# A quarter of the block copies behind VectorE's 32 by 32 transposes moves to GpSimd, in a hybrid decoder block

## The chip, the core and the metric

The kernel runs on one core of a Trainium2 chip (trn2). The metric is the device time of one execution in microseconds (us); of the kernel before, three runs are known (2516.44, 2516.70 and 2517.51), and one execution was taken with a profile. A core has TensorE (PE in the rows, its weight loads PEld), VectorE (DVE), ScalarE (ACT), GpSimd (POOL) and SyncE (SP), each with a queue of its own that it works through in order. A queue waits for another by semaphores.

## The reference

One decoder layer over 512 positions of width 2048, in float32:

```python
h = rmsnorm(x, norm_mix_g)
qa, ka, va, qb, kb, vb, ga, gb = split(h @ w_in)
ya = sliding_window_attention(qa, ka, va, sinks) @ w_branch_a    # window 128, 16 heads over 4 groups
yb = stick_breaking_attention(qb, kb, vb) @ w_branch_b           # strictly causal, 16 heads
x = x + (sigmoid(ga) * ya + sigmoid(gb) * yb) @ w_out
x = x + swiglu(rmsnorm(x, norm_ffn_g))
out = rmsnorm(x, norm_final_g)
```

Both attentions work in 128 by 128 blocks: a block of weights (query by key) has to be turned (key by query) before TensorE can multiply it with the values. The turning is what the change touches.

## The kernel before, in words

Every float32 product is made of three fp32r products: both factors are split into a high part (ScalarE casts it) and a low part (VectorE subtracts). For the weights this is `Weights.parts`: L153 casts a loaded chunk `raw` to `whi` on ScalarE, L154 makes `wlo` on VectorE. Three buffers of each let the two engines run up to two chunks ahead of TensorE; the cast of a chunk waits until TensorE has released the buffer. TensorE's stream of large products (lines L343 to L345 in the first half) is the main work. After each piece of it, `gap()` takes a waiting closure from the list `pieces`, so that the attention's small steps are written between the large products; `pace` says how many per piece. The final order on each engine is set by a scheduler that runs when the program is built and works from its own cost estimates, so a changed engine for one instruction can move others.

The first attention (`unit_a`, the stretch from about 105 to 370 us) has 28 turns of four 128 by 128 blocks: two `nc.vector.transpose` (L650) write `z`, in which every 32 by 32 block is turned in itself but still stands at its old place. `unblock` (L588 to L597) then makes 16 copies of 32 partitions each, which put the blocks in their place in `turned`. `split_turned` casts `turned` to `ph` (ScalarE, L601) and subtracts to get `pl` (VectorE, L602), and TensorE multiplies them with the values (L661, L662). Behind the last of these units TensorE goes on with the second attention: this is the hand-over, near 350 us.

The second attention (`head_b`, about 360 to 840 us) has 16 heads. `scores` makes sigmoids on ScalarE, two masks on GpSimd (`strictly_before`, L713), a scan and a product on VectorE; `turn(j)` transposes 4, 3, 2 or 1 blocks (L756), calls `unblock` with n = 4 to 1, casts to `ath` or `corner` (L601) and subtracts (L602); `values` are the products at L770 to L774. For the last group `pace` is raised, so that the pieces are done when the gates are: the heads stand closer together from about 750 us on.

A third user, `turn_x1` (L874), turns twelve column blocks of the residual (four blocks each) while the next product of the output matrix runs, about 1080 to 1185 us.

Which engine makes a copy is decided in `unblock`: of 16 copies `share` go to ScalarE, the others to VectorE. `share` is 10 in `unit_a` and 8 elsewhere:

```python
copy = nc.scalar.copy if (i + 1) * share // 16 > i * share // 16 else nc.vector.tensor_copy
copy(t4[c * Q : (c + 1) * Q, :, r], z4[r * Q : (r + 1) * Q, :, c])
```

Of the kernel before, what the change touches and what calls it, by code (L numbers as in the profile page):

```python
# [45 lines left out]
def kernel(  # L46
# [15 lines left out]
    nc = tc.nc  # L62
# [21 lines left out]
    def slot(s, dt=F32, w=T):  # L84
        return tp.tile([P, w], dt, tag="t", name=uid(s))
# [502 lines left out]
    def unblock(z, n, share):  # L588

        t = slot("turned")  # L590
        z4 = z[:, : n * P].rearrange("p (n c q) -> p n c q", n=n, c=4)
        t4 = t[:, : n * P].rearrange("p (n r q) -> p n r q", n=n, r=4)
        for i in range(16):
            r, c = i // 4, i % 4
            copy = nc.scalar.copy if (i + 1) * share // 16 > i * share // 16 else nc.vector.tensor_copy
            copy(t4[c * Q : (c + 1) * Q, :, r], z4[r * Q : (r + 1) * Q, :, c])  # L596
        return t  # L597

    def split_turned(z, n, hi, lo, share):
        t = unblock(z, n, share)[:, : n * P]  # L600
        nc.scalar.copy(hi, t)  # L601
        nc.vector.tensor_tensor(out=lo, in0=t, in1=f(hi), op=ALU.subtract)  # L602
# [271 lines left out]
    def turn_x1(k, xr, tag):  # L874

        g = gcol[:, KD + k : KD + k + 1]
        if k < KD - 4:
            z = slot("z")
            for t in range(NT):
                nc.vector.transpose(z[:, t * P : (t + 1) * P], xr[t][:, (k % 4) * P : (k % 4 + 1) * P])  # L880
            v = unblock(z, NT, 8)
            nc.scalar.activation(out=v, in_=v, func=AF.Copy, scale=g)
        else:
            b = bank(tag)
            for t in range(NT):
                transpose(b[:, t * P : (t + 1) * P], xr[t][:, (k % 4) * P : (k % 4 + 1) * P])
            v = slot("turned")
            nc.scalar.activation(out=v, in_=b, func=AF.Copy, scale=g)
        xs2[k] = v
        if k % 2 and k < KD // 2 + 2:  # L890
            forms_of(k // 2)
# [249 lines left out]
```

## Time and profile before

| | |
|---|---|
| median of three runs | 2516.7 us |
| the profiled execution, its own time | 2515.71 us |
| its span, first to last instruction | 2513.6 us |
| TensorE busy | 2472.4 us, 98% of the span |
| VectorE busy | 1977.8 us, 79% |
| ScalarE busy | 1377.9 us, 55% |
| GpSimd busy | 256.4 us, 10% |
| mean granted TensorE clock | 0.994 |
| copies of L596 | 888 on ScalarE, 776 on VectorE |

A row of a group gives the line, engine, operation and tiles, the count, the busy time, the mean duration of one in ns, and the idle time of the engine just before, with what ended it. In a timeline row the bracket holds the idle time before it and its releaser. TensorE's share says how much of the span it had a product in flight; where it waited, and for whom, stands in the list of waits.

### The profile page before, as it was taken

What the parts mean: (1) busy time and instruction counts of PE and PEld (TensorE: products, weight loads), DVE (VectorE), ACT (ScalarE), POOL (GpSimd) and SP (SyncE); (2) the same over time, 40 slices, a digit from 0 to 9 for tenths busy, and PEclk for the clock granted to TensorE, in tenths of its full rate; (3) what the DMA queues carried; (4) which work ended last, traced back from release to release, by engine and by line L of the source; (5) the groups of instructions that cost most, each with busy time, mean ns of one, the idle gap of its engine ahead of it and who ended that gap; (6) DMA issues with size and microseconds to landing.
All of it is one profiled execution on the core that took longest, in us unless ns stands there. A gap on an engine that the chain in (4) does not pass through costs nothing.

```text
span 2513.6 us, 33228 instructions
## 1 busy us (share of the span) xinstructions
PE 2472.4 (98%) x11529; PEld 2063.3 (82%) x11529; DVE 1977.8 (79%) x3457; ACT 1377.9 (55%) x2627; POOL 256.4 (10%) x490
## 2 busy tenths in 40 slices
PE   9999999999999999999999999999999999999997
PEld 8888978888887788888788888888888877888886
DVE  5688888988769644376788888888888878888888
ACT  6567776766657533265554555545555444333345
POOL 0000001111101000000000011000110033302100
PEclk9999999999999999999999999999999999999999
DMA  5332333333323644454456656566565699958652
GB/s 177 93 101 91 101 101 103 104 98 103 108 88 104 202 149 144 133 161 134 150 165 193 197 170 184 169 193 190 176 184 168 191 334 322 315 161 277 190 186 85
DMA packets 255784, 408.00 MB, mean 162 GB/s; under 512 B 16480, under 2 KB 103552, under 8 KB 255616
## 3 DMA queue, kind: packets, MB, share of 16 engines
q1 hardware_dynamic: 200944, 302.03, 38.7%
q0 software_dynamic: 47552, 91.25, 11.6%
q10 hardware_dynamic: 7120, 12.61, 1.3%
q8 instruction: 90, 1.47, 0.2%
q14 instruction: 78, 0.64, 0.1%
HBM read 344.48 MB, written 61.34 MB: 161 GB/s over the span
## 4 chain that ended last, share of the span: by engine, by line
PE 50%; issue 12%; POOL 2%; DVE 2%; DMA 1%; ACT 0%; POOLq 0%; DVEq 0%
PE mm L261 7%; PE mm L260 7%; PE mm L259 6%; PE at L260 5%; PE at L261 5%; PE at L259 5%; PE mm L345 3%; PE mm L343 3%; PE mm L344 3%; POOL fx L1031 2%; PE at L860 1%; PE mm L861 1%; PE mm L860 1%; PE at L861 1%; PE at L859 1%
## 5 line engine op out<-in xcount | busy, mean ns | idle before, releaser
L153 ACT CAST whi<-wx 128x1024 fp32r<-128x1024 f32 x256 | 269.6, 1053 | 306.5 <-PE mm L261 132.0
L260 PE MATMUL mm<-wlo,fx 128*128 128x512 f32 x1056 | 413.7, 392 | 1.1 <-DVE wlo L154 1.1
L261 PE MATMUL mm<-whi,fx 128*128 128x512 f32 x1056 | 411.9, 390 | 0.0
L154 DVE TENSOR_TENSOR wlo<-raw,whi 128x1024 fp32r<-128x1024 f32 (+1 forms) x209 | 253.7, 1215 | 186.1 <-ACT whi L153 184.4
L154 DVE TENSOR_TENSOR wlo<-wx,whi 128x1024 fp32r<-128x1024 f32 x256 | 312.6, 1222 | 80.5 <-ACT whi L153 80.1
L259 PE MATMUL mm<-whi,fx 128*128 128x512 f32 x1056 | 369.4, 390 | 0.4 <-ACT whi L153 0.4
L153 ACT CAST whi<-wz 128x1024 fp32r<-128x1024 f32 x198 | 207.7, 1054 | 281.1 <-PE at L261 111.4
L345 PE MATMUL mm<-fh,wlo 128*128 128x512 f32 x896 | 351.3, 392 | 3.8 <-DVE wlo L154 3.7
L343 PE MATMUL mm<-fh,whi 128*128 128x512 f32 x896 | 351.3, 392 | 0.0
L344 PE MATMUL mm<-fl,whi 128*128 128x512 f32 x896 | 351.0, 392 | 0.0
L153 ACT CAST whi<-raw 128x1024 fp32r<-128x1024 f32 (+1 forms) x209 | 218.2, 1046 | 222.9 <-PE mm L344 126.8
L260 PE MATMUL at<-wlo,fx 128*128 128x512 f32 x792 | 311.7, 394 | 4.1 <-DVE wlo L154 4.1
L261 PE MATMUL at<-whi,fx 128*128 128x512 f32 x792 | 309.6, 391 | 0.0
L596 ACT COPY turned<-z 32x128 f32<-32x128 f32 (+3 forms) x888 | 242.4, 273 | 110.3 <-DVE z L756 60.7
L154 DVE TENSOR_TENSOR wlo<-wz,whi 128x1024 fp32r<-128x1024 f32 x198 | 240.1, 1222 | 60.1 <-ACT whi L153 60.1
L259 PE MATMUL at<-whi,fx 128*128 128x512 f32 x792 | 277.9, 391 | 2.6 <-ACT whi L153 2.6
L260 PEld LDWEIGHTS mm<-wlo,fx 128*128 128x128 f32 x1056 | 198.6, 188 | 43.1 <-DVE wlo L154 2.2
L259 PEld LDWEIGHTS mm<-whi,fx 128*128 128x128 f32 x1056 | 198.0, 188 | 42.5 <-ACT whi L153 1.3
L261 PEld LDWEIGHTS mm<-whi,fx 128*128 128x128 f32 x1056 | 198.6, 188 | 40.9
L345 PEld LDWEIGHTS mm<-fh,wlo 128*128 128x128 f32 x896 | 169.3, 189 | 41.0 <-DVE wlo L154 5.5
L344 PEld LDWEIGHTS mm<-fl,whi 128*128 128x128 f32 x896 | 169.5, 189 | 33.4
L343 PEld LDWEIGHTS mm<-fh,whi 128*128 128x128 f32 x896 | 169.4, 189 | 33.1
(261 smaller groups left out, 4184.6 us busy)
## 6 DMA issues: line engine op xcount, KB each, us to landing
raw<-in_w_in_dram SPq DMA_DIRECT2D x135, 512.0 KB, 3.6
wz<-in_w_ffn_in_dram SPq DMA_DIRECT2D x88, 512.0 KB, 4.4
raw<-in_w_ffn_in_dram SPq DMA_DIRECT2D x83, 512.0 KB, 3.7
wx<-in_w_ffn_in_dram SPq DMA_DIRECT2D x49, 512.0 KB, 4.2
raw<-in_w_ffn_down_dram SPq DMA_DIRECT2D x44, 512.0 KB, 4.2
wz<-in_w_ffn_down_dram SPq DMA_DIRECT2D x44, 512.0 KB, 5.7
raw<-in_w_out_dram SPq DMA_DIRECT2D x32, 512.0 KB, 3.7
wx<-in_w_ffn_down_dram SPq DMA_DIRECT2D x22, 512.0 KB, 7.1
```

Of the source, the lines that this page charges most:

```text
L153: self.cast = nc.scalar.copy(hi[:, :n], raw[:, :n])
L154: nc.vector.tensor_tensor(out=lo[:, :n], in0=raw[:, :n], in1=f(hi[:, :n]), op=ALU.subtract)
L259: mm(banks[t], lhsT=hi, rhs=wh[:, kk, :], start=one, stop=False, skip_group_check=True)
L260: mm(banks[t], lhsT=hi, rhs=wl[:, kk, :], start=False, stop=False, skip_group_check=True)
L261: mm(banks[t], lhsT=lo, rhs=wh[:, kk, :], start=False, stop=end, skip_group_check=True)
L343: mm(b, lhsT=wh[:, kk, c], rhs=hi[k], start=(k == 0), stop=False)
L344: mm(b, lhsT=wh[:, kk, c], rhs=lo[k], start=False, stop=False)
L345: mm(b, lhsT=wl[:, kk, c], rhs=hi[k], start=False, stop=(k == nk - 1))
L596: copy(t4[c * Q : (c + 1) * Q, :, r], z4[r * Q : (r + 1) * Q, :, c])
L860: mm(banks[t], lhsT=hi[k][:, c], rhs=wl[:, kk, :], start=False, stop=False)
L861: mm(banks[t], lhsT=lo[k][:, c], rhs=wh[:, kk, :], start=False, stop=(k == nk - 1))
L1031: nc.gpsimd.dma_start(out=res[i][name], in_=form_d[p0 + i][name])
```

## The change

Of the 16 copies of a turn, the four with `i % 4 == n % 4` go to GpSimd, where `n` is the number of 128 by 128 blocks. As `i % 4` is the column of 32 in which the block stands in `z`, these are the four copies of one column.

```diff
         for i in range(16):
             r, c = i // 4, i % 4
             copy = nc.scalar.copy if (i + 1) * share // 16 > i * share // 16 else nc.vector.tensor_copy
+            if i % 4 == n % 4:
+                copy = nc.gpsimd.tensor_copy
             copy(t4[c * Q : (c + 1) * Q, :, r], z4[r * Q : (r + 1) * Q, :, c])
```

With `share` 10 and n = 4 (`unit_a`) GpSimd takes two copies of ScalarE's ten and two of VectorE's six. With `share` 8 the even `i` are VectorE's: n = 4 and n = 2 take four of VectorE's eight, n = 3 and n = 1 four of ScalarE's eight.

ScalarE at the hand-over, behind the splitting of the last keys of the first group (`kh`): the copies and casts of the last three turns of the first attention. Before:

```order
L509 CAST kh_3697<-v_3689 64x512
L153 CAST whi_3850<-raw_3848 128x1024
L596 COPY turned_3722<-z_3717 32x4x32 x10
L601 CAST ph_3720<-turned_3722 128x512
L664 COPY tmp_3758<-at_3753 64x512
L153 CAST whi_3904<-raw_3902 128x1024
L596 COPY turned_3787<-z_3782 32x4x32 x10
L601 CAST ph_3785<-turned_3787 128x512
```

Now (the lines behind the change are two higher):

```order
L509 CAST kh_3697<-v_3689 64x512
L153 CAST whi_3850<-raw_3848 128x1024
L598 COPY turned_3722<-z_3717 32x4x32 x8
L603 CAST ph_3720<-turned_3722 128x512
L666 COPY tmp_3758<-at_3753 64x512
L153 CAST whi_3904<-raw_3902 128x1024
L598 COPY turned_3787<-z_3782 32x4x32 x8
L603 CAST ph_3785<-turned_3787 128x512
```

Nothing changes its place here; two copies of ten are gone from each turn.

VectorE near the end of the second attention, from the low part of one weight chunk (`wlo_8640`) on. Before:

```order
L154 TENSOR_TENSOR wlo_8640<-raw_8637,whi_8639 128x1024
L602 TENSOR_TENSOR corner_2785<-turned_8536,corner_2784 128x128
L749 TENSOR_TENSOR a_8595<-a_8595,fl_8596 128x511
L602 TENSOR_TENSOR atl_8617<-turned_8618,ath_8616 128x512
L756 STREAM_TRANSPOSE z_8674<-a_8458 128x128
L756 STREAM_TRANSPOSE z_8674<-a_8402 128x128
L756 STREAM_TRANSPOSE z_8674<-a_8337 128x128
L154 TENSOR_TENSOR wlo_8729<-raw_8726,whi_8728 128x1024
L596 COPY turned_8680<-z_8674 32x3x32 x3
L748 SCALAR_TENSOR_TENSOR fl_8659<-fl_8659 128x384
L596 COPY turned_8680<-z_8674 32x3x32 x5
```

Now:

```order
L154 TENSOR_TENSOR wlo_8640<-raw_8637,whi_8639 128x1024
L604 TENSOR_TENSOR atl_8617<-turned_8618,ath_8616 128x512
L758 STREAM_TRANSPOSE z_8674<-a_8458 128x128
L758 STREAM_TRANSPOSE z_8674<-a_8402 128x128
L758 STREAM_TRANSPOSE z_8674<-a_8337 128x128
L750 SCALAR_TENSOR_TENSOR fl_8659<-fl_8659 128x384
L598 COPY turned_8680<-z_8674 32x3x32 x7
L751 TENSOR_TENSOR a_8658<-a_8658,fl_8659 128x383
L598 COPY turned_8680<-z_8674 32x3x32
L154 TENSOR_TENSOR wlo_8729<-raw_8726,whi_8728 128x1024
```

The next low part, `wlo_8729`, went from the place ahead of the eight copies to the place behind them and behind a scan.

ScalarE at the last head of the second attention (the turn into `turned_9121` is its first, with four blocks). Before:

```order
L596 COPY turned_9064<-z_9062 32x32 x8
L776 COPY tmp_9098<-at_9089 64x512
L601 CAST corner_2784<-turned_9064 128x128
L153 CAST whi_9142<-raw_9140 128x1024
L596 COPY turned_9121<-z_9114 32x4x32 x8
L781 DMA y_526<-yb_8842 128x512
L601 CAST ath_9119<-turned_9121 128x512
```

Now:

```order
L598 COPY turned_9064<-z_9062 32x32 x4
L603 CAST corner_2784<-turned_9064 128x128
L778 COPY tmp_9098<-at_9089 64x512
L598 COPY turned_9121<-z_9114 32x4x32 x8
L783 DMA y_526<-yb_8842 128x512
L153 CAST whi_9142<-raw_9140 128x1024
L603 CAST ath_9119<-turned_9121 128x512
```

The cast of the weight chunk moved from ahead of the eight copies to the place between them and the cast `ath` that the turn ends in.

## Rows read from the trace of the kernel before

**Rows 1.** Busy time by stretch: the stretch (us from the span's start), its length, busy us (and instructions) of PE, PEld, DVE, ACT and POOL, then the granted TensorE clock, the DMA share and GB/s. The hand-over, the middle and the end of the second attention, and the stage behind it with `turn_x1`.
```profile
315.00:370.00 55.00, 48.87 (x205) 38.91 (x204) 44.61 (x109) 41.26 (x100) 0.00 (x0) 0.97 0.28 87
...
370.00:750.00 380.00, 380.00 (x2002) 329.04 (x2001) 315.83 (x808) 251.36 (x656) 55.52 (x104) 1.00 0.33 104
...
750.00:840.00 90.00, 84.07 (x362) 67.95 (x361) 80.90 (x246) 65.13 (x192) 11.73 (x24) 0.94 0.31 100
...
840.00:1200.00 360.00, 360.00 (x1590) 298.10 (x1589) 195.03 (x418) 164.19 (x298) 6.62 (x12) 1.00 0.48 155
```

**Rows 2.** The waits of TensorE over the whole span, those of the first 840 us: who waited for whom, us in total, times, the longest.
```profile
PE at L661 <- ACT ph L601: 4.2, 1, 4.2
...
PE mm L345 <- DVE wlo L154: 3.7, 3, 1.8
...
PE at L773 <- ACT corner L601: 1.9, 2, 1.5
...
PE at L773 <- DVE corner L602: 1.2, 1, 1.2
...
PE at L662 <- DVE pl L602: 0.8, 1, 0.8
```

**Rows 3.** Timeline of the hand-over (start, us, engine, line, operation, tiles, count), ACT, DVE and the one long wait of PE.
```profile
338.40 3.07 ACT L596 COPY turned<-z 32x128 f32<-32x128 f32 x10 [2.76 <-DVE z L650]
...
341.49 1.05 ACT L153 CAST whi<-raw 128x1024 fp32r<-128x1024 f32 x1
...
342.57 1.23 DVE L154 TENSOR_TENSOR wlo<-raw,whi 128x1024 fp32r<-128x1024 f32 x1 [2.80 <-ACT whi L153]
...
353.03 0.77 DVE L650 STREAM_TRANSPOSE z<-s 128x256 f32<-128x256 f32 x2
...
353.73 1.18 DVE L154 TENSOR_TENSOR wlo<-raw,whi 128x1024 fp32r<-128x1024 f32 x1
...
353.83 3.06 ACT L596 COPY turned<-z 32x128 f32<-32x128 f32 x10 [1.00 <-DVE z L650]
...
356.92 0.62 ACT L601 CAST ph<-turned 128x512 fp32r<-128x512 f32 x1
...
357.59 0.80 PE L661 MATMUL at<-ph,vv 128*128 128x512 f32 x1 [4.18 <-ACT ph L601]
```

**Rows 4.** Timeline of the end of the second attention: a stall of TensorE at a weight chunk, with POOL.
```profile
796.38 1.42 POOL L713 TENSOR_SCALAR_AFFINE_SELECT a<-a 128x128 f32<-128x128 f32 x1
...
796.53 1.18 DVE L748 TENSOR_TENSOR_SCAN fl<-fl 128x512 f32<-128x512 f32 x1
...
797.63 1.16 DVE L596 COPY turned<-z 32x128 f32<-32x128 f32 x5
...
798.83 1.22 DVE L154 TENSOR_TENSOR wlo<-raw,whi 128x1024 fp32r<-128x1024 f32 x1
...
800.10 0.50 PE L345 MATMUL mm<-fh,wlo 128*128 128x512 f32 x1 [1.82 <-DVE wlo L154]
```

**Rows 5.** Groups by shape of the copies and of the casts and subtractions behind them, all turns: count, busy us, mean ns of one, idle before.
```profile
L596 ACT COPY turned<-z 32x128 f32<-32x128 f32 x504 | 149.3, 296 | 57.2 <-DVE z L650 31.7 <-DVE z L756 11.8 <-DVE z L880 4.1
...
L596 ACT COPY turned<-z 32x96 f32<-32x96 f32 x128 | 34.5, 269 | 15.0 <-DVE z L756 13.5
...
L596 ACT COPY turned<-z 32x32 f32<-32x32 f32 x128 | 27.6, 216 | 17.3 <-DVE z L756 16.0
...
L596 DVE COPY turned<-z 32x128 f32<-32x128 f32 x392 | 85.2, 217 | 5.2
...
L596 DVE COPY turned<-z 32x64 f32<-32x64 f32 x128 | 23.7, 185 | 1.7
...
L602 DVE TENSOR_TENSOR pl<-turned,ph 128x512 fp32r<-128x512 f32 x28 | 19.2, 687 | 10.3 <-ACT ph L601 10.2
...
L602 DVE TENSOR_TENSOR atl<-turned,ath 128x512 fp32r<-128x512 f32 x16 | 11.5, 719 | 0.3
```

**Rows 6.** GpSimd: a memset, two masks on an otherwise idle interface, the group of one kind of mask over the whole span (mean ns of one), and a mask that meets a subtraction with two inputs on VectorE (timeline rows and one group row).
```profile
242.71 0.21 POOL L718 MEMSET zero<- 128x128 f32 x1 [239.00 <-DVE q L498]
...
374.27 0.29 POOL L713 TENSOR_SCALAR_AFFINE_SELECT a<-a 128x128 f32<-128x128 f32 x1 [0.19 <-ACT a L746]
...
374.65 0.29 POOL L713 TENSOR_SCALAR_AFFINE_SELECT fl<-fl 128x128 f32<-128x128 f32 x1
...
L713 POOL TENSOR_SCALAR_AFFINE_SELECT fl<-fl 128x128 f32<-128x128 f32 x64 | 34.7, 542 | 500.7 <-ACT fl L744 479.5 <-issue 15.4 <-DVE turned L596 5.7
...
752.54 1.18 DVE L154 TENSOR_TENSOR wlo<-raw,whi 128x1024 fp32r<-128x1024 f32 x1
...
753.06 0.82 POOL L713 TENSOR_SCALAR_AFFINE_SELECT fl<-fl 128x128 f32<-128x128 f32 x1 [4.24 <-ACT fl L744]
...
753.64 0.37 DVE L602 TENSOR_TENSOR corner<-turned,corner 128x128 fp32r<-128x128 f32 x1
...
L602 DVE TENSOR_TENSOR corner<-turned,corner 128x128 fp32r<-128x128 f32 x16 | 4.6, 287 | 0.6 <-ACT corner L601 0.4
```

**Rows 7.** The waits between the engines at the hand-over (window 315 to 370 us): who waited for whom, us in total, times, the longest.
```profile
ACT turned L596 <- DVE z L650: 8.7, 4, 3.5
DVE wlo L154 <- ACT whi L153: 7.1, 4, 2.8
```

## The prediction, made before the changed kernel ran

> **What bounds the kernel now.** I read the busy time by stretch first, then TensorE's waits, then the timelines at those waits. TensorE is the bound nearly everywhere: in the middle of the second attention it is busy for all of 380 us while VectorE has 64 us and ScalarE 129 us to spare, and in the stage that holds the third user of the copies it is busy for all of 360 us [rows 1]. Whatever the copies cost there, nobody waits. Two stretches are different. At the hand-over from the first attention to the second, 315 to 370 us, TensorE idles 55.0 - 48.9 = 6.1 us and its granted clock is 0.97 of 2.4 GHz; at the end of the second attention, 750 to 840 us, it idles 90.0 - 84.1 = 5.9 us at 0.94 [rows 1]. The lower clock costs about 55 x 0.03 = 1.7 us and 90 x 0.06 = 5.4 us more (my estimates). So 6.1 + 5.9 + 1.7 + 5.4 = 19 us, 0.76%, is all that the two stretches can give back, and each wait there names ScalarE or VectorE: the largest is 4.2 us at L661 for the cast `ph` that ends a turn, then 3.7 us in three waits for `wlo`, 1.9 and 1.2 us for `corner` [rows 2].
>
> How the turn makes TensorE late is to be seen in the timeline of the hand-over. ScalarE makes ten copies in 3.07 us, then casts a weight chunk, and VectorE, idle for 2.80 us, waits for that cast; 15 us later ten copies from 353.83 end at 356.89, the cast `ph` follows at once, and TensorE, 4.18 us idle, starts when it ends [rows 3]. ScalarE waits for VectorE's transposes and VectorE for ScalarE's casts, four times each [rows 7]: one chain through both engines, in which ScalarE's copies are a link. At the end of the second attention the chain is VectorE's alone: it is busy 80.9 of 90 us [rows 1], and the stall at 800.10 is five copies and then `wlo` run after a scan without a gap [rows 4].
>
> **The change part by part.** 104 turns (28 + 64 + 12) give four copies each to GpSimd, 416 in all. VectorE is spared 28 x 2 + (16 + 16 + 12) x 4 = 232 of them, ScalarE 28 x 2 + (16 + 16) x 4 = 184. Only those in the two stretches can show.
>
> *What one copy costs on GpSimd* the trace doesn't show. Nearest are its memset of 128x128, 0.21 us, and its mask of 128x128, 0.29 us when VectorE leaves it alone, with starts 0.38 us apart; the masks' mean is 0.54 us, and one beside a VectorE scan with two inputs took 1.42 us [rows 4, 6]. A mask reads and writes as a copy does, so I take 0.38 to 0.54 us: four copies in 1.5 to 2.2 us, with ends at 0.8 and 5.7 us. ScalarE's eight take 8 x 0.296 = 2.4 us [rows 5], so GpSimd is not the last to finish, unless it must first wait for a `wlo` such as that at 353.73 [rows 3].
>
> *What a GpSimd copy costs VectorE.* The mask at 753.06 begins inside a `wlo` and ends 0.16 us after it: GpSimd stands still until VectorE is done. The other way VectorE loses little: the subtraction beside that mask took 0.37 us where its group has 0.287, and `atl`, which meets masks, has 0.719 where `pl` of the same shape, which meets none, has 0.687 [rows 5, 6]. So 0.03 to 0.08 us per meeting; nothing below it, since a meeting frees nothing. I take 0.06.
>
> By the Trainium skill, SBUF — State Buffer, section Who interferes with whom, VectorE and GpSimd share one pair of SBUF ports as an exclusive lock: a GpSimd instruction that has it keeps a VectorE copy, or an instruction with two SBUF inputs, out until it ends. The mask that waited for `wlo` agrees; the 0.08 us that the subtraction lost does not look like a wait for a whole mask. By the rule VectorE would lose more than it is spared; the price of that is the second rival's, below, from rows alone.
>
> *Hand-over.* In each turn ScalarE makes 8 copies in place of 10: 2 x 0.296 = 0.59 us. Four turns stand in the chain [rows 7], 2.4 us at most; nothing where VectorE's or GpSimd's copies end last. I take three of four, -1.8 us (0 to -2.4). The order of ScalarE is as it was there. TensorE's product with `ph` stands two products earlier than before, which moves the wait and not its end. The clock stays down as long as a wait of some 2.4 us is left; I take 0 (0 to -1.7).
>
> *End of the second attention.* A head gives away 4 x 0.217 + 4 x 0.185 = 1.6 us of VectorE's time (n = 4 and 2) and pays 16 x 0.06 = 1.0 us: -0.6 us, for three heads before the last stalls -1.9 us [rows 5]. The four copies that ScalarE loses at n = 3 and n = 1 (4 x 0.269 and 4 x 0.216) lie beside VectorE's eight and give nothing. The moved casts take part of it back: `wlo_8729` now ends about 3 us later, behind eight copies and a scan, and at the last head the cast of a chunk (1.05 us [rows 3]) stands between the copies and `ath`. I charge +0.9 us: -1.0 in sum (-2.8 to +1.0), clock 0 (-5.4 to +2).
>
> *Elsewhere.* In the first attention before 315 us and in the middle of the second TensorE doesn't wait; what hides the copies is that weight chunks are ready up to two ahead. If that lead were used up, each turn would cost what it delays `wlo`, under 1 us. GpSimd's queue now has masks behind copies: the scan waits for the masks, and is late only if four copies take longer than VectorE's own copies, `wlo`, `atl` and transposes in between, over 4 us. The stores of the residual, which GpSimd issues, stand behind the copies of `turn_x1`; nothing reads them for hundreds of us. Cost 0.
>
> Sum: -1.8 - 1.0 = -2.8 us on the profiled execution's 2515.7 us (span 2513.6 and 2.1 around it), which is 1.0 us under the median of the runs: **2513.9 us**. From no change a measurement of this kernel tells about 0.2%, 5 us; this forecast is inside that.
>
> **The rivals.**
>
> 1. *The relief adds up.* If the delay at the hand-over was gathered over many more turns than four, each spared 0.59 us, the whole 6.1 + 1.7 us goes, and at the end, with one stall less, half of 5.4 us of clock and 1.9 us: 2516.7 - 12.4 = 2504.3 us. For it: the two engines wait on each other in every late turn [rows 7]. Against it: ScalarE's casts also wait for TensorE to release buffers, so a lead is capped and lost again.
>
> 2. *GpSimd's copies hold VectorE up for their whole length* (the other side). Place: the same two stretches. Each copy of 0.29 us [rows 6] would cost VectorE 0.29: per head 16 x 0.29 - 1.6 = +3.0 us, three heads +9; at the hand-over 4 x (4 x 0.29 - 2 x 0.217) = +2.9 us: 2516.7 + 12 = 2528.6 us. It decides from 1.6 / 16 = 0.10 us per copy on, near the 0.08 of the subtraction. Against it: `atl` against `pl`, +0.03.
>
> 3. *Nothing reaches TensorE*: GpSimd's copies end when ScalarE's used to, and the turn is as long as before: 2516.7 us.
>
> That the copies stay where they were is out: the order shows eight of ten on ScalarE, and the rest on GpSimd.
>
> **How the numbers follow.** The forecast gets 0.47, between its bounds from 2510.5 (-2.4 and -2.8, with part of the clock) to 2517.5; of it 0.07 lies beyond 0.2%. Rival 1 gets 0.22, rival 2 0.13 (0.02 of that within 0.2%, where it only just decides), rival 3 0.18. Faster by over 0.2%: 0.07 + 0.22 = 0.29. Slower by over 0.2%: 0.11. Within: 0.40 + 0.18 + 0.02 = 0.60. The range of 8 in 10 runs from 2506.5, which leaves about half of rival 1 out, to 2521, which leaves the heavier half of rival 2 out; the forecast's own range is 2510.5 to 2517.5.
>
> **What would show it.** Right: 416 GpSimd copies with a mean of 0.4 to 0.55 us; ScalarE's copies of a late turn in 2.45 us; the wait at L661 near 350 us at 2 to 3 us; VectorE's copies of 32x128 at 0.22 to 0.28 us. Wrong towards faster: no wait at all between 315 and 370 us and a clock of 1.00 there. Wrong towards slower: VectorE's copies or subtractions longer by 0.1 us or more, GpSimd copies of over 0.6 us with `ph` and `ath` waiting for them, or TensorE waiting for `wlo` between 370 and 750 us, where it never did.

## The result, and the profile after

The changed kernel takes 2502.65 us (median of four runs, 2501.10 to 2503.84) against 2516.57 us for the kernel before (four runs, 2512.58 to 2517.51): a ratio of 0.9945, 95% interval 0.9933 to 0.9957. The forecast of 2513.9 us, and the low end of its range at 2506.5, lie above that. The profiled execution took 2503.35 us, its span is 2501.6 us, 12.0 us shorter than before.

Busy time by stretch after the change (the columns of [rows 1]):

```profile
315.00:370.00 55.00, 55.00 (x247) 45.62 (x246) 46.31 (x100) 41.31 (x95) 14.68 (x34) 1.00 0.34 107
370.00:750.00 380.00, 380.00 (x2002) 329.10 (x2001) 304.90 (x717) 231.64 (x567) 115.33 (x296) 1.00 0.32 101
750.00:840.00 90.00, 82.89 (x367) 67.80 (x366) 75.08 (x209) 56.50 (x150) 28.18 (x80) 0.96 0.42 137
840.00:1200.00 360.00, 360.00 (x1598) 298.34 (x1598) 189.16 (x367) 164.46 (x303) 25.30 (x64) 1.00 0.47 156
```

The hand-over is full: 55 of 55 us at a clock of 1.00, where 6.1 us were idle. The end of the second attention is still not: 7.1 us idle where there were 5.9. The two stretches that had no wait have none now.

TensorE's waits of the first 840 us (columns as in [rows 2]):

```profile
PE at L775 <- ACT ath L603: 4.1, 1, 4.1
...
PE mm L345 <- DVE wlo L154: 1.6, 2, 1.0
...
PE at L772 <- ACT ath L603: 0.9, 1, 0.9
...
PE at L775 <- DVE corner L604: 0.3, 1, 0.3
PE at L775 <- ACT corner L603: 0.2, 1, 0.2
```

The waits for `ph` and `pl` are gone, that for `corner` on ScalarE fell from 1.9 to 0.2 us, the stall of [rows 4] from 1.82 to 1.01, and a new one of 4.1 us for `ath` has come at the end of the second attention.

The turn that made TensorE wait 4.18 us in [rows 3], after the change (timeline; code lines are two higher):

```profile
344.43 0.77 DVE L652 STREAM_TRANSPOSE z<-s 128x256 f32<-128x256 f32 x2
345.13 1.18 DVE L154 TENSOR_TENSOR wlo<-raw,whi 128x1024 fp32r<-128x1024 f32 x1
345.24 2.45 ACT L598 COPY turned<-z 32x128 f32<-32x128 f32 x8 [0.99 <-DVE z L652]
345.34 2.11 POOL L598 COPY turned<-z 32x128 f32<-32x128 f32 x4 [13.55 <-DVE z L652]
...
347.77 0.62 ACT L603 CAST ph<-turned 128x512 fp32r<-128x512 f32 x1
...
349.16 0.39 PE L663 MATMUL at<-ph,vv 128*128 128x512 f32 x1
```

From the start of the transposes to that of the cast it takes 3.34 us where it took 3.89 (353.03 to 356.92), the 0.6 us that the two copies were priced at. But the transposes now begin at 344.43 where they began at 353.03. What changed is not this turn but when it starts. The waits between the two engines at the hand-over still stand, not much shorter than in [rows 7]:

```profile
ACT turned L598 <- DVE z L652: 7.2, 4, 2.8
DVE wlo L154 <- ACT whi L153: 5.9, 3, 2.4
```

The copies by shape (columns as in [rows 5]):

```profile
L598 POOL COPY turned<-z 32x128 f32<-32x128 f32 x224 | 83.8, 374 | 359.0 <-DVE z L652 163.7 <-ACT whi L153 100.9 <-issue 28.2
L598 DVE COPY turned<-z 32x128 f32<-32x128 f32 x224 | 57.8, 258 | 4.1
...
L598 POOL COPY turned<-z 32x96 f32<-32x96 f32 x64 | 25.9, 404 | 18.9 <-DVE z L758 14.1 <-PE mm L345 1.2 <-PE mm L344 0.6
...
L598 POOL COPY turned<-z 32x64 f32<-32x64 f32 x64 | 17.8, 279 | 30.3 <-DVE z L758 27.1 <-POOL a L715 1.1
...
L598 POOL COPY turned<-z 32x32 f32<-32x32 f32 x64 | 16.9, 264 | 8.7 <-DVE z L758 5.8 <-PE mm L345 0.2 <-POOL a L715 0.2
```

A GpSimd copy has a mean of 0.26 to 0.40 us; VectorE's own 32x128 copies went from 217 to 258 ns; the subtractions `pl` and `atl` of 128x512 did not move (687 and 718 ns), but no `pl` meets a GpSimd copy in the trace, and `atl` meets masks alone, as before.

**Where the 12.0 us lie.** The weight chunks come in the same order in both traces, so the start of TensorE's first product with each chunk's low part can be set against its counterpart. That shift is -0.54 us before the first copy of a turn; it grows by -8.94 between 318 and 387 us (of the time before), by -1.72 between 753 and 873 us, and by -0.8 later, at waits for weights near 2040 to 2120 us. The first and last lie at places without such copies, and vary by as much from run to run below; what caused them was not looked for.

The 8.94 us are 6.13 us of idle time, 1.5 to 1.75 us of clock, and a rest of 1.1 to 1.3. The clock is read from slices of five us of the kernel before, behind its 4.18 us wait:

```profile
355.00:360.00 5.00, 2.41 (x6) 1.93 (x7) 3.51 (x13) 4.84 (x14) 0.00 (x0) 0.71 0.33 105
360.00:365.00 5.00, 5.00 (x23) 4.11 (x22) 4.71 (x14) 3.44 (x11) 0.00 (x0) 0.94 0.22 62
```

5 x 0.29 + 5 x 0.06 = 1.75 us, which counts some time in which TensorE still idled; by the starts of its products, mostly 0.43 us apart there and 0.23 later, it is 1.5 us. The rest is not itemised; a part of it is that the last product before each stop counts as busy for 0.39 us where in a full stream the next starts after some 0.23.

### The profile page after: what moved, and what is told of

Same layout as the page of the kernel before. It is cut to its first block, busy times and chain, and to the rows that moved or that the text cites. A ratio compares the mean times of both kernels' runs of the same rounds, so it can differ in the third digit from the quotient of the medians.

```text
span 2501.6 us, 33308 instructions
## 1 busy us (share of the span) xinstructions
PE 2466.5 (99%) x11529; PEld 2060.9 (82%) x11529; DVE 1950.7 (78%) x3225; ACT 1333.8 (53%) x2443; POOL 396.0 (16%) x906
## 3 DMA queue, kind: packets, MB, share of 16 engines
q0 software_dynamic: 47552, 91.25, 11.6%
## 4 chain that ended last, share of the span: by engine, by line
PE 49%; issue 13%; POOL 2%; DVE 2%; DMA 1%; ACT 0%; POOLq 0%; DVEq 0%; ACTq 0%
PE mm L261 6%; PE mm L260 6%; PE mm L259 6%; PE at L260 5%; PE at L261 5%; PE at L259 5%; PE mm L345 3%; PE mm L343 3%; PE mm L344 3%; POOL fx L1033 2%; PE at L862 1%; PE mm L863 1%; PE mm L862 1%; PE at L863 1%; PE at L861 1%
## 5 line engine op out<-in xcount | busy, mean ns | idle before, releaser
L598 ACT COPY turned<-z 32x128 f32<-32x128 f32 (+1 forms) x704 | 194.8, 277 | 100.3 <-DVE z L758 55.2
L598 POOL COPY turned<-z 32x128 f32<-32x128 f32 (+3 forms) x416 | 144.4, 347 | 417.0 <-DVE z L652 163.7
```

## The experiments

Theory: **the relief is gathered.** Each turn gives a little to ScalarE and VectorE; it is kept as a lead of the weight chunks before TensorE needs them, and spent when the hand-over would stall. Rival: **only the late turns count**, as the prediction had it. The lead is the time from the end of VectorE's subtraction `wlo` to the start of TensorE's first product with it. All kernels are set against the one before by the shift of TensorE's stream over the hand-over, counted from the start of the first attention, since the total also holds 1 to 3 us of chance elsewhere. The copies of a turn in the first attention are given as ScalarE / VectorE / GpSimd; the lead is at three chunks that TensorE needs at 250, 300 and 318 us of the time before:

```
kernel              copies    lead at 250  300  318   shift over the hand-over
before              10/6/0         1.6     1.5  1.4     0
changed              8/4/4         6.0     7.3  8.0    -8.9
first_only           8/4/4         5.9     7.3  7.9    -8.9
first_first24        8/4/4 *       6.0     7.3  7.9    -7.5   (* in the first 24 turns)
first_scalar2        8/6/2         4.7     5.7  6.0    -5.2
first_even8          8/8/0         1.9     2.5  3.0    -3.0
first_last4          8/4/4 *       1.6     1.4  1.3    -0.7   (* in the last 4 turns)
first_vector2       10/4/2         1.8     0.4  0.4    +1.6
wide8                6/2/8         7.4     6.9 12.5    +6.0
```

### Only the last four turns

Edit of the kernel before (`turns` counts calls of `unblock`; the change's own line, with a condition):

```diff
+            if 24 < turns[0] <= 28 and i % 4 == n % 4:
+                copy = nc.gpsimd.tensor_copy
```

> GpSimd makes its four copies only in the last four of the first attention's 28 turns; all else as before. Theory 'gathered' (every one of the 28 turns that is spared copies adds to the lead of the weight chunks, and the hand-over wait shows the sum): four turns give 4 x 0.3 to 0.6 us, so the wait at L661 near 357 us falls from 4.2 to 2 to 3 us, the waits for wlo near 325 us stay, and the span falls by 1 to 2.5 us (2513.6 to about 2511.5). Theory 'last turns' (only the turns in the chain at the hand-over count, and what the others are spared is lost again): most of the 8.9 us comes already here, span 2505 to 2507.

Measured: 2513.68 us, one run. TensorE's waits in this kernel, 315 to 372 us:

```profile
PE at L665 <- ACT ph L605: 3.7, 1, 3.7
PE mm L345 <- DVE wlo L154: 1.0, 1, 1.0
PE at L666 <- DVE pl L606: 0.8, 1, 0.8
```

The late turns have the change's copies, and the stalls are still there: 4.2 us became 3.7, a shift of -0.7 us. Two of the four turns, which start at 337.6 and 353.0 us in the kernel before, run ahead of the long wait, the other two behind it; two turns at the prediction's 0.59 us would give at most 1.2.

### Only the first 24 turns

```diff
+            if turns[0] <= 24 and i % 4 == n % 4:
+                copy = nc.gpsimd.tensor_copy
```

> GpSimd makes its four copies only in the first 24 of the first attention's 28 turns; the last four and the second attention as before. Theory 'gathered': 24 of 28 parts of the lead are there, so no wait near 325 us, and at L661 at most 1 us is left; span 2504 to 2507. Theory 'last turns': the waits from 325 to 357 us stay nearly as before (5 to 6 us in all); span 2511 to 2513.

Measured: 2507.98 us, one run; TensorE's waits in the same window:

```profile
PE at L665 <- ACT ph L605: 0.8, 2, 0.6
```

The 24 turns give -7.5 of the -8.9 us. The last two of them start at 322.9 and 329.6 us in the kernel before, among the stalls, but the lead at 318 us, ahead of both, already is the changed kernel's. Gathered it is; the rival is out.

Two limits. The first three turns don't count: the leads at 145 and 152 us, made by 141 us, are the same in both kernels, 10.0 and 11.9 us. The difference at 318 us comes from the 19 turns that start between 142 and 307 us. And the scheduler wrote a new order for ScalarE and VectorE from about 172 us on (earlier in first_even8 and wide8) in every kernel that changes the early turns, while first_last4 keeps the old one up to the hand-over. Where the order is the old one, spared copies alone do gather: the chunk that TensorE needs at 176 us, split before the orders part, has 1.5 us more lead than before, and from 262 to 318 us, where ScalarE's order is the old one again, the gain grows from 5.1 to 6.6 us. What the new order gave in between no run separates.

### One engine's share alone

Only ScalarE's two of the four, then only VectorE's two:

```diff
+            if share == 10 and i % 8 == 4:      # first_scalar2
+            if share == 10 and i % 8 == 0:      # first_vector2
+                copy = nc.gpsimd.tensor_copy
```

> In the first attention's turns GpSimd takes only ScalarE's two copies (ScalarE 8, VectorE 6, GpSimd 2); second attention as before. Theory 'ScalarE's link' (in each late turn ScalarE's copies are the link of the chain): nearly the whole 8.9 us, span 2504 to 2506, lead of wlo as in the changed kernel. Theory 'VectorE's share' (VectorE's load is what is short): under 2 us, span 2511 to 2513.

> In the first attention's turns GpSimd takes only VectorE's two copies (ScalarE 10, VectorE 4, GpSimd 2); second attention as before. Theory 'ScalarE's link': under 2 us, span 2511 to 2513. Theory 'VectorE's share': 28 x 2 x 0.22 = 12 us less VectorE work, nearly the whole 8.9 us, span 2504 to 2506.

Measured: 2507.50 us and 2516.64 us, one run each; shifts of -5.2 and +1.6. Without VectorE's copies a wait of 2.2 us for `ph` is left; without ScalarE's, the waits are as long as before:

```profile
PE at L663 <- ACT ph L603: 3.2, 1, 3.2
PE mm L345 <- DVE wlo L154: 2.9, 1, 2.9
```

(the last kernel, 315 to 372 us). The parts don't add up: VectorE's two are worth nothing alone, and -3.7 us on top of ScalarE's. That VectorE's alone even lost 1.6 us is not explained; its order was written anew by the scheduler.

### Less on ScalarE without GpSimd

```diff
-            split_turned(z, NT, ph, pl, 10)
+            split_turned(z, NT, ph, pl, 8)
```

> No copy on GpSimd. In the first attention ScalarE makes eight copies and VectorE eight (before: ten and six), so ScalarE is spared the same 0.59 us per turn that the change spares it and VectorE pays 2 x 0.217 = 0.43 us. Theory (ScalarE's length of a turn is the link, GpSimd is only the place where the copies go): about what ScalarE's two alone gave, -5.2 us, so 2511 to 2512 us. Rival (what counts is the work of both engines together, since each waits for the other in turn, so the copies have to leave both): 2 x 0.296 - 2 x 0.217 = 0.16 us per turn, 0 to -1 us, 2515.5 to 2516.5 us, with VectorE's wlo late in place of ScalarE's ph.

Measured: 2510.61 us, one run; -3.0 us over the hand-over, between the two expectations. Two copies moved from ScalarE to VectorE are worth 3.0, to GpSimd 5.2, and two more from VectorE to GpSimd again 3.7. So both engines' time counts, ScalarE's more, as far as the new orders allow a comparison.

### The two halves of the change

```diff
-            if i % 4 == n % 4:
+            if share == 8 and i % 4 == n % 4:       # second_only
+            if share == 10 and i % 4 == n % 4:      # first_only
```

> GpSimd takes its four copies only in the second attention and in the turning of the residual; the first attention keeps ScalarE's ten and VectorE's six. Theory (the two stretches gain independently: 8.9 us at the hand-over, 1.7 us at the end of the second attention): 2516.5 - 1.7 = 2514.8 us, with the wait of about 4.2 us for ph at the hand-over still there and the new wait of about 4 us for ath near 813 us too. Rival (the end of the second attention gained only because the first attention handed over with more weights made ahead): 2516.5 us, and the stalls of the end as before.

> GpSimd takes its four copies only in the first attention; the second attention and the turning of the residual are as before. Theory (two stretches that gain apart from each other): 8.9 us at the hand-over with no wait left between 315 and 370 us, and nothing at the end of the second attention: 2516.6 - 8.9 = 2507.7 us, and together with the run of the other part alone (2513.8 us) the changed kernel's gain. Rival (the hand-over gains as much because GpSimd's work in the second attention also unloads the first heads there): 2509 us or more, with a wait left near 357 us.

Measured: 2513.80 us and 2504.68 us, one run each. The second attention alone shifts by nothing at the hand-over, where the waits for `ph` (4.2 us) and `pl` (0.8 us) stand, and by -1.0 us at 840 us; the first alone by -8.9 at the hand-over, and by nothing at the end. Added up they are 9.9 us, against 8.9 + 1.7 = 10.6 for the change: independent within 0.7 us, and 1.0 us at the end where 1.7 was expected. The 4.1 us wait for `ath` stands in second_only, as expected. The total of first_only is 3 us better than expected, through shifts of 1.7 us in stages that it leaves alone, and because the expectation started from a median 0.9 us above the profiled execution of before.

### The end of the second attention: who ends the turn

The new wait there, in the changed kernel:

```profile
810.83 1.11 ACT L598 COPY turned<-z 32x96 f32<-32x96 f32 x4 [1.98 <-DVE z L758]
810.83 1.99 DVE L598 COPY turned<-z 32x96 f32<-32x96 f32 x8
810.85 1.20 POOL L598 COPY turned<-z 32x96 f32<-32x96 f32 x4 [4.75 <-DVE z L758]
811.96 1.04 ACT L153 CAST whi<-raw 128x1024 fp32r<-128x1024 f32 x1
812.92 0.51 ACT L603 CAST ath<-turned 128x384 fp32r<-128x384 f32 x1
...
813.49 0.69 PE L775 MATMUL at<-ath,vv 128*128 128x384 f32 x1 [4.09 <-ACT ath L603]
```

ScalarE has four copies and VectorE eight, GpSimd having taken ScalarE's; between ScalarE's copies and `ath` stands the cast of a weight chunk. Three other allotments were run, all with the changed kernel's first attention:

```diff
-            if i % 4 == n % 4:
+            if i % 4 == (0 if n == 4 else 2):                        # second_vector: 8/4/4
+            if i % 4 == 0 if share == 10 else i % 8 in (0, 3):       # second_two:    6/6/4
+            if i % 4 == 0 or share == 8 and i % 8 == 3:              # second_three:  6/4/6
```

> As the changed kernel, but in the second attention's turns of three and one blocks GpSimd takes four of VectorE's eight copies where it took four of ScalarE's. Theory (the new 4.1 us wait for ath near 813 us is ScalarE waiting for VectorE's eight copies of a three-block turn): VectorE is spared 4 x 0.24 + 4 x 0.17 = 1.6 us more per head, the wait shrinks to under 2 us and the stretch from 750 to 840 us gains 2 to 3 us over the changed kernel: about 2500 us. Rival (the wait comes from the order that the scheduler wrote, with VectorE's scan and low part ahead of the copies): it stays within 1 us of the changed kernel, 2502.5 us. Rival (ScalarE with its eight copies of 0.27 us then ends last): 2503 to 2505 us.

> As the changed kernel in the first attention; in the second, GpSimd takes two of ScalarE's eight copies and two of VectorE's eight in every turn, so that a turn of three blocks is 6 x 0.27 = 1.6 us on ScalarE, 6 x 0.25 = 1.5 us on VectorE and 1.2 to 1.6 us on GpSimd. Theory (at the end of the second attention the turn's longest engine sets ath and corner): the copies of a turn end about 0.5 us earlier than in the changed kernel (eight on VectorE, 2.0 us) and than with GpSimd always on VectorE's copies (eight on ScalarE, 2.2 us); three late turns, 1 to 2 us, about 2501 us. Rival (the order in which the scheduler puts weight casts ahead of ath decides): 2502.5 us, within 1 us of either.

> As second_two, but in the second attention GpSimd takes four of VectorE's copies and two of ScalarE's (six in all, ScalarE six, VectorE four). Theory (GpSimd needs 1.6 us for four copies and 3.35 us for eight by the traces, so some 2.4 us for six, longer than ScalarE's six at 1.6 us): GpSimd ends the turn last, masks wait behind it, and it is 0 to 3 us slower than second_two. Rival (VectorE's busy time sets the end of the second attention, whoever ends the turn): VectorE is spared two more copies per turn, 4 x 2 x 0.22 = 1.8 us per head, 2500 us or less.

Measured, four runs each: 2502.45 us (2502.35 to 2502.69), ratio 0.9943 (0.9927 to 0.9960); 2502.78 us (2502.54 to 2503.78), ratio 0.9946 (0.9930 to 0.9963); **2495.43 us** (2494.30 to 2496.44), ratio 0.9916 (0.9901 to 0.9931). The first two are the changed kernel's time; the expected 2 to 3 and 1 to 2 us are not in it. In second_vector the wait for `ath` shrank to 1.9 us, but waits for `corner` of 2.3 and 1.2 us came back ahead of it. The rivals that named the scheduler's order, at 2502.5 us, have the time right. In second_two every engine has done with the turn by 811.0 us, and `ath` begins behind the weight cast, so `ath` is as late there without VectorE's eight copies:

```profile
809.32 1.67 ACT L598 COPY turned<-z 32x96 f32<-32x96 f32 x6 [1.98 <-DVE z L758]
...
811.01 1.04 ACT L153 CAST whi<-raw 128x1024 fp32r<-128x1024 f32 x1
811.96 0.51 ACT L603 CAST ath<-turned 128x384 fp32r<-128x384 f32 x1
...
812.52 0.69 PE L775 MATMUL at<-ath,vv 128*128 128x384 f32 x1 [4.64 <-ACT ath L603]
```

The third beats both kernels, by 7.2 us the changed one. Its busy time at the end:

```profile
750.00:840.00 90.00, 90.00 (x413) 75.17 (x412) 72.75 (x183) 59.89 (x157) 40.24 (x110) 1.00 0.46 154
```

TensorE does not wait between 315 and 840 us in it. Over the end of the second attention it shifts by -11.6 us against the kernel before, where the changed kernel has -1.7, second_two -2.4 and second_vector -2.9. Why is open. It is not VectorE's time alone, as the rival had it: second_vector leaves VectorE the same four copies. Nor is it enough that both engines are spared: second_two spares both. second_three spares VectorE four copies and ScalarE two, and the scheduler's order is another; no run separates the amount from the order. My expectation there fell. GpSimd does end late turns last, with six copies, and it doesn't matter:

```profile
794.36 1.52 ACT L598 COPY turned<-z 32x64 f32<-32x64 f32 x6 [1.31 <-DVE z L758]
794.45 1.95 POOL L598 COPY turned<-z 32x64 f32<-32x64 f32 x6 [0.39 <-PE mm L345]
...
796.43 0.41 ACT L603 CAST ath<-turned 128x256 fp32r<-128x256 f32 x1 [0.55 <-POOL turned L598]
```

The lead of the weight chunks, 6 to 10 us there where the kernel before falls to 0.1, takes it up.

### Eight copies on GpSimd

Relative to the changed kernel; the second attention is second_vector's:

```diff
-            if i % 4 == n % 4:
+            if share == 10 and i % 4 in (0, 1) or share == 8 and i % 4 == (0 if n == 4 else 2):
```

> As second_vector, and in the first attention GpSimd takes eight copies of the sixteen (ScalarE five, VectorE three), in 8 x 0.28 to 0.40 us = 2.2 to 3.2 us per turn. Theory (the relief gathers over the turns, and all of it that TensorE could get back at the hand-over is had by the change already, since no wait is left there): the first 370 us are as in second_vector, within 0.5 us. Rival (GpSimd now ends the turn last, at 3.2 us against ScalarE's 2.4 before): the casts ph come later, waits between 315 and 370 us come back, +2 to +6 us.

Measured: 2519.99 us (ten runs, 2517.64 to 2521.92), ratio to before 1.0014 (1.0005 to 1.0024), and 17.5 us over second_vector. By the code GpSimd leaves ScalarE six copies and VectorE two, not the five and three expected. The rival was right in kind, and low: over the hand-over wide8 is 15 us behind second_vector. Here GpSimd ends the turn, and by more than the lead can hide (timeline of the late turn):

```profile
356.53 1.82 ACT L598 COPY turned<-z 32x128 f32<-32x128 f32 x6 [0.81 <-DVE z L652]
356.63 3.43 POOL L598 COPY turned<-z 32x128 f32<-32x128 f32 x8 [3.38 <-DVE z L652]
...
360.09 0.62 ACT L603 CAST ph<-turned 128x512 fp32r<-128x512 f32 x1 [1.74 <-POOL turned L598]
...
360.76 0.80 PE L663 MATMUL at<-ph,vv 128*128 128x512 f32 x1 [5.45 <-ACT ph L603]
```

Eight copies take 3.35 us in the mean of the first 25 turns (2.6 to 4.4); four take 1.60 in the changed kernel. The next weights lie ready 13 us ahead, and TensorE waits for `ph`: the lead of the weights says when a stall comes only while the weights' chain is the late one.

## Why the prediction was wrong

- **The bound: near.** The stretches put at no wait have none, and the other two hold what can be had. They were put at 19 us; second_three gained 8.9 + 11.6 = 20.5 us in them, the clock's share and the rest that is not itemised included.
- **GpSimd's copy: near.** Taken at 0.38 to 0.54 us, measured at 0.26 to 0.40 by shape; four end within 1.60 us of the first's start in the mean of the first attention's turns (1.26 to 2.55), as forecast (1.5 to 2.2), so that ScalarE's eight at 2.45 us are the longer in the mean.
- **VectorE's loss: the size right, the kind not.** 0.06 us per GpSimd copy was charged. VectorE's 32x128 copies lost 41 ns each, those of 32x64 39 (185 to 224). The charge came from a VectorE that hardly waits; the trace shows one that does wait, but for short copies (last section). So the second rival's price, a whole 0.29 us per copy, did not come, and GpSimd's copies are those that stretch most, up to 1.28 us where the shortest took 0.20. By the exclusive lock of the Trainium skill (SBUF — State Buffer, Who interferes with whom) whoever issues first keeps the other out to its end. The trace agrees in both directions, but for about the last 0.14 us of a GpSimd copy.
- **The hand-over: the step that failed.** "Four turns stand in the chain", 2.4 us at most, took the window in which the stalls are seen for the window in which they are made. [rows 7] counted the links inside 55 us and gave the end of the range from that; the first attention had turned blocks since 104 us, and the lead of `wlo` fell from 11.9 us at 152 us to 4.5 at 201 and 1.4 at 318, and no view of waits shows a lead that has not yet run out. The last four turns alone are worth 0.7 us (first_last4), less than was charged; the 24 before them 7.5 (first_first24), and at 318 us the changed kernel's lead is 8.0. The first rival had this mechanism, 6.1 + 1.7 = 7.8 us; it got 0.22 because a lead "is capped and lost again" when casts wait for buffers. That fits up to 152 us, where both kernels have the same lead. Behind it the lead was far from a cap: from 200 to 318 us it was 1.3 to 6.6 us, and in the changed kernel 5 to 10 us. The sign that the prediction named for this case, no wait and a clock of 1.00 between 315 and 370 us, is what came. How little ScalarE's casts of weights waited for TensorE to release a buffer stands in the waits of the kernel before, 152 to 318 us:

```profile
ACT whi L153 <- PE mm L344: 0.4, 1, 0.4
```

- **The clock at the hand-over: wrong with it.** 0 was taken, 1.5 to 1.75 us came back. That it stays down as long as a wait of some 2.4 us is left does not hold: first_even8 has one of 2.55 us at 1.00.
- **The end of the second attention: the size right, by luck.** -1.0 was forecast, from less waiting; -1.7 came, with more of it. TensorE's idle time there rose from 5.9 to 7.1 us: less for `wlo` (2.7 to 1.6 us in this stretch) and `corner` (3.1 to 0.5), and then 5.0 us for `ath` (0.2 before). What got shorter is the time at the lower clock, a gain that the sum took at 0: by the slices of five us below 1.00 it cost at most 5.2 us before, and 3.5 after (last section). About 1.2 us more are not itemised. As foreseen a weight cast stands ahead of `ath`, but at the turn of three blocks; that part of the order was not looked at. Here the first rival, which expected 4.6 us, was the wrong one. The slices of the kernel before:

```profile
800.00:805.00 5.00, 4.90 (x16) 4.00 (x17) 4.79 (x17) 4.03 (x11) 0.62 (x2) 0.66 0.36 108
...
815.00:820.00 5.00, 2.35 (x10) 1.81 (x9) 4.66 (x20) 4.80 (x16) 0.00 (x0) 0.79 0.42 154
820.00:825.00 5.00, 5.00 (x13) 3.87 (x13) 4.45 (x15) 3.45 (x12) 0.00 (x0) 0.52 0.49 157
```

- **Nothing reaches TensorE (third rival): no.** But first_vector2 is such a case: two copies fewer on VectorE, and no gain.

## What to carry to other kernels

Before pricing a small saving on a chain that feeds the bound engine, read how far ahead of need its products are, turn by turn, from the last point at which that lead was full: a saving per turn counts in every turn since then, not in those where the stall is seen. Where two engines wait on each other in turn, price the relief of both together, since one alone may show nothing. A third engine can be given work as long as what it does in a turn stays near the others' share; in this kernel four of sixteen copies fitted in the first attention and six in the second, and eight in the first did not. Where a scheduler rewrites the order with every edit, compare the orders before a gain is put down to the spared work.

## What the runs showed of the hardware

GpSimd's copies depend on what VectorE does beside them, and VectorE's on GpSimd's. In the late turn above four GpSimd copies took 2.11 us beside a `wlo`; nine us later, beside copies of VectorE, they took 1.26. Single copies of these two turns, and the later turn's four together:

```profile
345.34 1.13 POOL L598 COPY turned<-z 32x128 f32<-32x128 f32 x1 [13.55 <-DVE z L652]
...
354.53 1.26 POOL L598 COPY turned<-z 32x128 f32<-32x128 f32 x4 [3.35 <-DVE z L652]
...
354.67 0.23 DVE L598 COPY turned<-z 32x128 f32<-32x128 f32 x1
354.86 0.28 POOL L598 COPY turned<-z 32x128 f32<-32x128 f32 x1
354.91 0.32 DVE L598 COPY turned<-z 32x128 f32<-32x128 f32 x1
```

The copy of 1.13 us begins inside the `wlo` that ends at 346.31 and ends 0.16 us behind it. All eleven GpSimd copies of this shape that begin inside a `wlo` end 0.15 us behind it: they wait for VectorE. VectorE waits too. Its copy of 0.32 us began when GpSimd's had 0.23 us to go; alone it takes 0.22. Those that began with 0.14 us to go, or less, took 0.22 to 0.23. Of the `wlo` that began inside a GpSimd copy the longest took 1.30 us, where the others take 1.22. So in these meetings the second to begin waits for the first, and VectorE loses less because a GpSimd copy, at 0.28 us, is over sooner than a `wlo`.

The clock does not follow from the length of one wait. In the changed kernel the 4.09 us wait has a granted clock of 0.53 in its five us, and 0.78 in the next:

```profile
810.00:815.00 5.00, 1.51 (x4) 1.32 (x5) 4.65 (x16) 2.55 (x6) 1.08 (x4) 0.53 0.33 105
815.00:820.00 5.00, 5.00 (x21) 4.10 (x20) 3.10 (x16) 3.86 (x15) 1.77 (x8) 0.78 0.35 105
```

In the kernel before, the 1.82 us stall of [rows 4] was followed by 0.66 in 800 to 805 us, while first_even8 kept 1.00 from 345 to 365 us with a wait of 2.55 us in it. What tells these apart stays open.
